# Gate and up of the second token half by seven products of quarters instead of eight

## The chip, the cores and the metric

The kernel runs on one core of one Trainium2 chip. The metric is the device time of one execution in microseconds (us). Before the change the median of three runs is 1322.51 us (1320.72 to 1323.11).

## What is computed

One encoder layer on 1024 tokens of width 1024, all in float32. The change lies in its last part, the feed-forward network (FFN) with a hidden width of 2816:

```python
x = x + jnp.concatenate([out_a, out_b], axis=-1) @ w_out[l]
h2 = rmsnorm(x, norm2_w[l])
x = x + (jax.nn.silu(h2 @ w_gate[l]) * (h2 @ w_up[l])) @ w_down[l]
```

Ahead of it stand a norm, one input projection (`w_in`), sparse attention with a top-k choice of keys, and a retention recurrence. `out_a` and `out_b` are the outputs of the last two.

## The kernel before

**Precision.** TensorE multiplies in a rounded format (`F32R`), so every operand is split in two: `hi`, the rounded copy that ScalarE (ACT) writes, and `lo`, the remainder, which VectorE (DVE) gets as source minus `hi`. A product is then three matmuls: hi times hi, hi times lo, lo times hi. Each unit of 128 rows and 128 columns of a stationary operand is loaded anew for every matmul.

**Stages.** The tokens form eight blocks of 128, in two halves of four. The stages follow one another: `in_proj(0)`, `in_proj(1)`, `out_proj(0)`, `ffn(0)`, `out_proj(1)`, `ffn(1)`. Attention, selection and retention are threads of their own that run between the matmuls of these stages; attention of the second half ends in the last group of `ffn(0)`, where `last()` waits for it and `out_prep` makes the inputs of `out_proj(1)` and loads the residual `x1` of blocks 4 to 7 (L974).

**FFN (L1013).** The split, transposed activations of a half lie in `Thi` and `Tlo` (eight slices of 128 model columns by 512 tokens). The 22 tiles of 128 hidden columns go in `groups` of 4, 4, 4, 4, 4 and 2. For a hidden tile `j`, gate and up are 2 x 8 x 3 = 48 matmuls with 512 token columns each (only tile 0 does them in two halves of 256 columns). Then the silu follows: tanh on ACT, two operations on DVE, and the split of the hidden tile, `hh` on ACT and `hl` on DVE. After a group its part of the down projection runs: per hidden tile 24 matmuls of 512 columns, and eight additions of 512 columns to `x1` for the group. In the last group each sum goes out by a DMA from ACT's queue.

**Norm (L1000).** `out_proj` (L982) goes over four chunks of `w_out`; behind the last chunk, `norm2(b)` squares and scales block `b`, and a returned function transposes it (8 matmuls against `eye`) and splits it into `Thi` and `Tlo` with eight 128-column operations on ACT and eight on DVE (`scale_in`, L328).

**Weights.** Raw weights come by SP's DMA queue into `wraw` (three buffers). `pieces` (L273) splits them in steps of 512 columns per partition into a pair `whi`, `wlo`, of which there are two (L261). `weights()` (L912) hands out the pair that is ready and starts the next chunk's filling, so the kernel works exactly one chunk ahead: a chunk can be split only when the matmuls of the chunk before last have read their pair. A gate and up chunk is one hidden tile.

**Order.** Filling a chunk is a thread (`w`) that `tick()` (L872) steps between matmuls, by a model of the engines' backlog (`charge`, L800). The framework that turns these calls into instructions then orders each engine's instructions; the rows show that this order is not that of the calls. Memory comes from pools: `per` lives through the kernel, `s12` and `s34` are the stages' own. PSUM (eight banks) has three banks `d` for products, three `t`, and two for `l` in the second stage pool.

Of the kernel before, what the change touches and what calls it, by code (L numbers as in the profile page):

```python
# [16 lines left out]
NB = 8  # L17
KT = 8
H = 8
# [99 lines left out]
class Layer:  # L119
    def __init__(self, tc, a, out, stack):  # L120
# [9 lines left out]
        self.per = pool("per", bufs=1)  # L130

# [18 lines left out]

    def st(self, shape, dt=F32, tag=None, bufs=1):
        return self.new(self.stage, shape, dt, tag, bufs)
# [4 lines left out]
    def junk(self):  # L157
        return self.sb([128, 1024], BF16, tag="junk")
# [53 lines left out]
    def constants2(self):  # L212
# [14 lines left out]
        self.bits = self.sb([128, 32], U32, tag="bits")  # L227
# [4 lines left out]
    def bias_tables(self):  # L232

        nc, a = self.nc, self.a
        far = self.sb([128, 8], tag="far")
        nc.scalar.dma_start(far, a["rel_bias"][15:16, :].to_broadcast([128, 8]))
        bias = self.sb([128, H, 256], tag="bias")
# [35 lines left out]
    def pieces(self, loads, step, n, rows):  # L273
# [7 lines left out]
        def fill():  # L281
            late = None
            for i, parts in enumerate(loads):
# [4 lines left out]
                raw = self.sb([128, 1024], tag=tag, bufs=bufs)[:, :step * n].rearrange("p (k n) -> p k n", n=n)  # L288
# [6 lines left out]
                for k0 in range(0, step, sub):  # L295
# [9 lines left out]
                    yield  # L305
            late()
# [33 lines left out]
    def x_load(self, b, queues):  # L340
        xr = self.xr[b] = [self.sb([128, 512], tag="mb_", bufs=8) for _ in range(2)]
# [61 lines left out]
    def post_idx(self, b, p):  # L403
# [6 lines left out]
        if b >= 2:  # L410
            self.iq[b] = self.sb([128, 128], tag="iq", bufs=4)
            nc.vector.tensor_copy(self.iq[b], ci[:, 128:256])
# [41 lines left out]
    def post_q(self, b, c, p):  # L454
        nc = self.nc
        if c == 0:
            self.until(lambda: b < 4 or b - 4 in self.qused, *self.threads)
            self.q[b] = self.sb([128, 512], tag="q", bufs=4)
# [116 lines left out]
    def scores(self, b):  # L575
# [4 lines left out]
        dup = self.sb([128, 512], tag="rl", bufs=2)  # L580
# [7 lines left out]
        iqT = self.sb([128, 512], F32R, tag="iqT", bufs=1)  # L588
# [6 lines left out]
        sc = self.sb([128, 1024], tag="sc", bufs=2)[:, :n]  # L595
        self.sc[b] = sc
        for c0 in range(0, n, 512):
            w = min(512, n - c0)
            for h in range(4):
                p = self.pt(w)  # L600
                nc.tensor.matmul(p, iqT[:, h * 128:h * 128 + 128], self.ikT[:, c0:c0 + w], start=True, stop=True)
                rl = self.sb([128, 512], tag="rl", bufs=2)[:, :w]
# [76 lines left out]
    def attention(self, b):  # L679
# [6 lines left out]
        qT = self.sb([128, 1024], F32R, tag="qT", bufs=1)  # L686
# [22 lines left out]
        for hp in range(H // 2):  # L709
            bias = self.bias[:, 2 * hp:2 * hp + 2, 256 - near:]  # L710
            if b >= 2:
                mb = self.sb([128, 2, 256], tag="mb")
# [27 lines left out]
            for j0 in range(0, b + 1, 2):  # L740
# [6 lines left out]
                ph = self.sb([128, 512], F32R, tag="ph", bufs=2)[:, :nj * 256]  # L747
                plo = self.sb([128, 512], F32R, tag="plo", bufs=2)[:, :nj * 256]
# [11 lines left out]
        wide = self.sb([128, 512], tag="rl", bufs=2)  # L760
# [10 lines left out]
    def heads_out(self, b, hp, pa):  # L771
# [3 lines left out]
        t = self.sb([128, 128], tag="oT")  # L775
# [120 lines left out]
    def plan(self):  # L896
# [77 lines left out]
    def out_prep(self, b):  # L974
# [3 lines left out]
        self.x1[b] = [self.mtile("ma", b), self.mtile("mb", b)]  # L978
        for s in range(2):
            nc.sync.dma_start(self.x1[b][s], self.x[b * 128:(b + 1) * 128, 512 * s:512 * s + 512])  # L980

    def out_proj(self, half):  # L982
        nc = self.nc
        bs = [4 * half + i for i in range(4)]
        late = []
        for c in range(4):
            w = self.weights()
            for b in bs:
# [5 lines left out]
                if c == 3:  # L994
                    late.append(self.norm2(b))
                    if b % 4 in (1, 2, 3):
                        late.pop(0)()
        return late

    def norm2(self, b):  # L1000
# [8 lines left out]
        for s in range(2):  # L1009
            nc.vector.tensor_scalar(xn[:, 512 * s:512 * s + 512], x1[s], rs, None, op0=OP.mult)  # L1010
        return lambda: [self.transpose_in(xn[:, 512 * g:512 * g + 512], b % 4, g, self.n2) for g in range(2)]

    def ffn(self, half, late, last):  # L1013
        nc = self.nc
        for j0, g in self.groups:
# [25 lines left out]
            for c in range(2):  # L1041
                hi, lo = self.weights()
                for t0 in (0, 2):
                    ps = [self.pd(), self.pd()]
                    for js in (range(g - 1), range(g - 1, g)):
                        for i in range(2):
                            ts = slice(128 * (t0 + i), 128 * (t0 + i) + 128)
                            for j in js:
                                nc.tensor.matmul(ps[i], hh[:, j, ts], hi[:, j, :], start=(j == 0), stop=False)
                                nc.tensor.matmul(ps[i], hh[:, j, ts], lo[:, j, :], start=False, stop=False)  # L1050
# [107 lines left out]
```

## Time and profile before

| | |
|---|---|
| median of 3 runs | 1322.51 us |
| the profiled execution | 1322.34 us, of which the span of its instructions 1320.6 us |
| TensorE matmuls (PE) | 1290.5 us busy, 98% |
| weight loads (PEld) | 1119.0 us, 85%, beside the matmuls |
| VectorE (DVE) | 889.4 us, 67% |
| ScalarE (ACT) | 723.3 us, 55% |
| GpSimd (POOL) | 57.5 us, 4% |
| granted TensorE clock | 0.998 of full speed |
| second `out_proj` | from 895.1 us, second FFN from 944.6 us to the end |

Busy times overlap. A matmul's duration holds its way through the array, so matmuls that follow one another overlap too, and the pace of a run of them (its length over its count) says what one costs. All instructions carry the line of a helper, L99, so rows are told apart by the names of their tiles.

### The profile page before, as it was taken

The page shows a single profiled execution, that of the slowest core. Times are in us where ns is not written, and L with a number is a line of the kernel's source. Part 1 is how long each engine was busy: PE and PEld are TensorE (multiplying, and loading weights), DVE is VectorE, ACT ScalarE, POOL GpSimd, SP SyncE. Part 2 cuts the span into 40 slices and gives each one's busy share as a digit, 9 for nine tenths or more (in the row PEclk, how much of TensorE's full clock was granted, in tenths as well). Part 3 has the DMA queues.
Part 4 walks back from the last instruction along what each step waited for, and adds up shares of the span by engine and source line. Part 5 has one row for each costly group of instructions (what it writes and reads, how often), then busy time and mean ns, then how long its engine had stood idle before and what let it go on. Part 6 is the DMA issues. An engine that isn't in the chain of part 4 may idle for free.

```text
span 1320.6 us, 21083 instructions
## 1 busy us (share of the span) xinstructions
PE 1290.5 (98%) x7619; PEld 1119.0 (85%) x7619; DVE 889.4 (67%) x2536; ACT 723.3 (55%) x1706; POOL 57.5 (4%) x68
## 2 busy tenths in 40 slices
PE   8799998999999999999999999999999999999998
PEld 7799898999999978888888878889988888888886
DVE  6679899789978877877887775554634343434343
ACT  7778877556685787578569734332532323232221
POOL 1401011010020000000000000000000000000000
PEclk9999999999999999999999999999999999999999
DMA  8433224221341322322322232245233333333331
GB/s 276 145 81 97 58 62 111 65 65 33 93 122 59 89 65 87 96 64 65 96 75 78 72 89 72 64 128 177 72 105 96 96 96 96 94 91 94 90 93 66
DMA packets 157785, 121.24 MB, mean 92 GB/s; under 512 B 8176, under 2 KB 137840, under 8 KB 157552
## 3 DMA queue, kind: packets, MB, share of 16 engines
q1 hardware_dynamic: 151744, 111.14, 28.8%
q10 hardware_dynamic: 5936, 8.74, 1.9%
q8 instruction: 60, 0.98, 0.3%
q14 instruction: 45, 0.37, 0.1%
HBM read 115.67 MB, written 4.19 MB: 91 GB/s over the span
## 4 chain that ended last, share of the span: by engine, by line
PE 74%; DVE 12%; ACT 8%; issue 2%; DMA 2%; POOL 2%; ACTq 0%; SPq 0%; DVEq 0%; POOLq 0%
PE d L99 64%; PE t L99 8%; ACT junk L99 3%; DVE wlo L99 2%; PE l L99 2%; DVE L L99 1%; ACT whi L99 1%; ACT Thi L99 1%; DMA bias<-in_near_dram 1%; ACT waste L99 1%; DVE zqk L99 0%; DVE plo L99 0%; DMA mb__101<-in_xt_dram 0%; DVE junk L99 0%; DVE tr L99 0%
## 5 line engine op out<-in xcount | busy, mean ns | idle before, releaser
L99 ACT ACTIVATE whi<-wraw 128x512 fp32r<-128x512 f32 (+1 forms) x388 | 220.7, 617 | 253.5 <-PE d L99 181.9
L99 PE MATMUL d<-Thi,whi 128*128 128x512 f32 (+1 forms) x736 | 284.7, 387 | 0.0
L99 PE MATMUL d<-whi,Thi 128*128 128x256 f32 (+1 forms) x960 | 281.6, 294 | 3.1 <-ACT Thi L99 1.2
L99 PE MATMUL d<-Tlo,whi 128*128 128x512 f32 (+1 forms) x736 | 283.9, 386 | 0.5 <-DVE Tlo L99 0.4
L99 PE MATMUL d<-Thi,wlo 128*128 128x512 f32 (+1 forms) x736 | 283.7, 386 | 0.0
L99 PE MATMUL d<-wlo,Thi 128*128 128x256 f32 (+1 forms) x960 | 272.3, 284 | 1.4 <-DVE wlo L99 1.3
L99 PE MATMUL d<-whi,Tlo 128*128 128x256 f32 (+1 forms) x960 | 272.1, 284 | 0.0
L99 DVE TENSOR_TENSOR wlo<-wraw,whi 128x512 fp32r<-128x512 f32 (+1 forms) x390 | 251.9, 677 | 6.5 <-ACT whi L99 5.6
L99 PEld LDWEIGHTS d<-whi,Thi 128*128 128x128 f32 x960 | 182.2, 190 | 7.8 <-ACT Thi L99 2.1
L99 PEld LDWEIGHTS d<-wlo,Thi 128*128 128x128 f32 x960 | 182.4, 190 | 3.2 <-DVE wlo L99 2.3
L99 ACT ACTIVATE junk<-sc,tc 128x384 bf16<-128x384 f32 (+5 forms) x186 | 163.6, 879 | 34.2 <-DVE tc L99 30.2
L99 PEld LDWEIGHTS d<-whi,Tlo 128*128 128x128 f32 x960 | 182.1, 190 | 0.0
L99 PEld LDWEIGHTS d<-Thi,wlo 128*128 128x128 f32 x736 | 138.2, 188 | 30.1
L99 PEld LDWEIGHTS d<-Tlo,whi 128*128 128x128 f32 x736 | 138.4, 188 | 28.6 <-DVE Tlo L99 1.1
L99 PEld LDWEIGHTS d<-Thi,whi 128*128 128x128 f32 x736 | 138.1, 188 | 28.1 <-ACT Thi L99 0.3
L99 PE MATMUL d<-whi,hh 128*128 128x512 f32 x352 | 140.1, 398 | 0.9 <-DVE mb__5825 L99 0.9
L99 PE MATMUL d<-wlo,hh 128*128 128x512 f32 x352 | 139.1, 396 | 0.0
L99 PE MATMUL d<-whi,hl 128*128 128x512 f32 x352 | 138.7, 396 | 0.0
L99 DVE TENSOR_TENSOR th<-th,d 128x512 f32<-128x512 f32 x44 | 30.2, 685 | 98.2 <-PE d L99 98.1
L99 PEld LDWEIGHTS d<-whi,hh 128*128 128x128 f32 x352 | 66.1, 188 | 16.8 <-DVE mb__5825 L99 1.4
L99 PEld LDWEIGHTS d<-whi,hl 128*128 128x128 f32 x352 | 66.1, 188 | 16.0
L99 PEld LDWEIGHTS d<-wlo,hh 128*128 128x128 f32 x352 | 66.2, 188 | 15.0
(304 smaller groups left out, 1731.7 us busy)
## 6 DMA issues: line engine op xcount, KB each, us to landing
wraw<-in_w_gate_dram SPq DMA_DIRECT2D x88, 256.0 KB, 3.1
wraw<-in_w_up_dram SPq DMA_DIRECT2D x88, 256.0 KB, 3.5
wraw<-in_w_down_dram SPq DMA_DIRECT2D x44, 512.0 KB, 3.9
wraw<-in_w_in_dram SPq DMA_DIRECT2D x24, 512.0 KB, 3.8
wraw<-in_w_in_dram SPq DMA_DIRECT2D x32, 256.0 KB, 3.4
wraw<-in_w_out_dram SPq DMA_DIRECT2D x16, 512.0 KB, 4.1
maA<-in_x_dram SPq DMA_DIRECT2D x20, 256.0 KB, 5.1
wraw<-in_w_in_dram SPq DMA_DIRECT2D x7, 292.0 KB, 3.3
```

The source lines that it names most:

```text
L99: return f(*args, **kw)
```

## The change

For the second half gate and up go by Strassen's scheme (its form with fifteen additions). For a pair of hidden tiles the weights are taken as two by two quarters (512 model columns by 128 hidden columns, gate beside up) and the activations as two by two quarters (512 model columns by 256 tokens). Seven products of sums of quarters stand in for the eight products of quarters; each has 2 x 4 x 3 = 24 matmuls with 256 token columns. The activations' sums and splits are made once, in `Phi` and `Plo` (seven each, by `turned`). The weights' sums are made per pair by `factor`, and each factor is split in one operation of 1024 columns on ACT and one on DVE; a chunk of weights is two factors. Products are partly added up in PSUM and partly by copies on ACT and additions on DVE. The raw quarters come as 512-column `quad` tiles, six buffers, by the same number of bytes as before. `hh` and `hl` now lie, twice, in the memory of `Thi` and `Tlo`. Blocks go through `out_proj` in the order 4, 6, 5, 7. `ffn(0)` stays as it was; its down projection becomes the function `down`, with the same lines.

Tiles of attention and of the earlier stages move from `per` to a pool `early`, which ends with `ffn(0)`; a new stage pool `s5` takes its memory. `x1` of blocks 4 to 7 has tiles of its own in `s5`, and its eight loads are called behind `ffn(0)` instead of within its last group. PSUM has six banks `d` and two `t` in the new stage. In the diff below, further tiles that only change `sb` into `at_` are left out.

```diff
+    def at_(self, shape, dt=F32, tag=None, bufs=1):
+        return self.new(self.early, shape, dt, tag, bufs)
...
+    def quad(self, pr, n):
+        got = self.quads.setdefault(pr, [])
+        while len(got) < n and pr < NH // 2:
+            r, c = divmod(len(got), 2)
+            q = self.st([128, 2, 4, 128], tag="quad", bufs=6)
+            for u, w in enumerate((self.w_gate, self.w_up)):
+                self.nc.sync.dma_start(q[:, u], w[512 * c:512 * c + 512, 256 * pr + 128 * r:256 * pr + 128 * r + 128]
+                                       .rearrange("(k p) n -> p k n", p=128))
+            got.append(q)
+        return got
+    def factor(self, pr, m):
+        nc = self.nc
+        q = self.quad(pr, 4)
+        if m == 0:
+            self.quad(pr + 1, 2)
+        new = lambda: self.st([128, 2, 4, 128], tag="S", bufs=2)
+        add = lambda out, a, b, op: nc.vector.tensor_tensor(out, a, b, op=op)
+        if m == 2:
+            self.s1, self.s2 = new(), new()
+            add(self.s1, q[2], q[3], OP.add)
+            add(self.s2, self.s1, q[0], OP.subtract)
+            return self.s2
+        if m == 3:
+            return self.s1
+        if m == 4:
+            s3 = new()
+            add(s3, q[0], q[2], OP.subtract)
+            return s3
+        if m == 5:
+            add(self.s2, q[1], self.s2, OP.subtract)
+            return self.s2
+        return q[{0: 0, 1: 1, 6: 3}[m]]
...
+    def chunk_parts(self, items):
+        nc = self.nc
+        hi, lo = [t[:, :1024 * len(items)].rearrange("p (i u k n) -> p i u k n", u=2, k=4, n=128) for t in self.wpair()]
+        def fill():
+            late = None
+            for i, (pr, m) in enumerate(items):
+                if late:
+                    late()
+                src = self.factor(pr, m)
+                nc.scalar.activation(hi[:, i], src, AF.Copy)
+                late = lambda i=i, src=src: nc.vector.tensor_tensor(lo[:, i], src, hi[:, i].bitcast(F32), op=OP.subtract)
+                if m in (5, 6):
+                    self.quad(pr + 1, m - 2)
+                yield
+            late()
+        return (hi, lo), fill()
...
-                for j in range(g):
-                    yield gu(j0 + j)
+                if half == 0:
+                    for j in range(g):
+                        yield gu(j0 + j)
+                else:
+                    parts = [(j0 // 2 + i, m) for i in range(g // 2) for m in range(7)]
+                    for i in range(0, len(parts), 2):
+                        yield lambda i=i, parts=parts: self.chunk_parts(parts[i:i + 2])
...
-        self.x1[b] = [self.mtile("ma", b), self.mtile("mb", b)]
+    def x1_load(self, b, tiles):
+        self.x1[b] = tiles
...
+            self.nc.sync.dma_start(self.x1[b][s], self.x[b * 128:(b + 1) * 128, 512 * s:512 * s + 512])
...
-                    late.append(self.norm2(b))
-                    if b % 4 in (1, 2, 3):
+                    late.append(norm(b))
+                    if len(late) > 1:
...
+        if b >= 4:
+            return lambda: self.turned(b, xn)
...
+    def split_part(self, m, t, src):
+        c = slice(128 * t, 128 * t + 128)
+        self.nc.scalar.activation(self.Phi[:, m, :, c], src, AF.Copy)
+        self.nc.vector.tensor_tensor(self.Plo[:, m, :, c], src, self.Phi[:, m, :, c].bitcast(F32), op=OP.subtract)
+    def turned(self, b, xn):
+        nc = self.nc
+        x = self.st([128, 8, 128], tag="cc", bufs=2)
+        for g in range(2):
+            p = self.pt()
+            for k in range(4):
+                nc.tensor.transpose(p[:, k * 128:k * 128 + 128], xn[:, 512 * g + k * 128:512 * g + k * 128 + 128], self.eye)
+            nc.vector.tensor_tensor(x[:, 4 * g:4 * g + 4, :], p.rearrange("p (k n) -> p k n", n=128),
+                                    self.n2[:, 4 * g:4 * g + 4, None].to_broadcast([128, 4, 128]), op=OP.mult)
+        if b < 6:
+            self.xa = x
+            for g in range(2):
+                self.split_part(g, b - 4, x[:, 4 * g:4 * g + 4, :])
+            return
+        (a1, a2), (b1, b2) = [(y[:, 0:4, :], y[:, 4:8, :]) for y in (self.xa, x)]
+        t1, t2, t3, t4 = [self.st([128, 4, 128], tag=n) for n in ("u2", "u3", "p5", "th")]
+        sub = lambda out, p, q: nc.vector.tensor_tensor(out, p, q, op=OP.subtract)
+        sub(t1, b1, a1)
+        sub(t2, b2, t1)
+        self.split_part(2, b - 6, t2)
+        self.split_part(3, b - 6, t1)
+        sub(t3, b2, b1)
+        self.split_part(4, b - 6, t3)
+        sub(t4, a2, t2)
+        self.split_part(5, b - 6, b2)
+        self.split_part(6, b - 6, t4)
...
+    def gate_up(self, part, late, hh, hl):
+        nc = self.nc
+        flat = lambda c: c.rearrange("p i n -> p (i n)")
+        two = lambda p: p.rearrange("p (u n) -> p u n", n=256)
+        keep = lambda name: self.st([128, 2, 256], tag=name)
+        for m in range(7):
+            hi, lo = part()
+            if m in (0, 1, 3):
+                bank = two(self.pd())
+                if m == 0:
+                    X = bank
+                if m == 3:
+                    Z = bank
+            else:
+                bank = Z if m == 5 else X
+            for u in range(2):
+                for k in range(4):
+                    first = m in (0, 1, 3) and u == 0 and k == 0
+                    for i, (w, t) in enumerate(((hi, self.Phi), (hi, self.Plo), (lo, self.Phi))):
+                        nc.tensor.matmul(bank[:, u, :], w[:, u, k, :], t[:, m, k, :], start=first and i == 0,
+                                         stop=(k == 3 and i == 2), skip_group_check=True)
+                    self.tick()
+                if m == 1 and u == 0 and late:
+                    late.pop(0)()
+            self.evacuate()
+            if m == 0:
+                p1 = keep("p1")
+                nc.scalar.activation(p1, X, AF.Copy)
+            elif m == 1:
+                c1 = self.st([128, 2, 2, 256], tag="cc", bufs=2)
+                nc.vector.tensor_tensor(c1[:, :, 0, :], bank, p1, op=OP.add)
+            elif m == 2:
+                u2 = keep("u2")
+                nc.scalar.activation(u2, X, AF.Copy)
+            elif m == 3:
+                p5 = keep("p5")
+                nc.scalar.activation(p5, Z, AF.Copy)
+            elif m == 4:
+                u3 = keep("u3")
+                nc.scalar.activation(u3, X, AF.Copy)
+                c2 = self.st([128, 2, 2, 256], tag="cc", bufs=2)
+                nc.vector.tensor_tensor(c2[:, :, 1, :], u3, p5, op=OP.add)
+            elif m == 5:
+                nc.vector.tensor_tensor(c1[:, :, 1, :], Z, u2, op=OP.add)
+                self.silu(flat(c1[:, 0]), flat(c1[:, 1]), hh[:, 0, :], hl[:, 0, :])
+            else:
+                nc.scalar.activation(c2[:, :, 0, :], X, AF.Copy)
+                self.silu(flat(c2[:, 0]), flat(c2[:, 1]), hh[:, 1, :], hl[:, 1, :])
...
+    def ffn_fast(self, late):
+        both = [self.sb([128, 4096], F32R, tag=t).rearrange("p (i j n) -> p i j n", i=2, n=512) for t in ("Thi", "Tlo")]
+        for i, (j0, g) in enumerate(self.groups):
+            hh, hl = [t[:, i % 2] for t in both]
+            ready = []
+            def part():
+                if not ready:
+                    hi, lo = self.weights()
+                    ready.extend((hi[:, i], lo[:, i]) for i in range(hi.shape[1]))
+                return ready.pop(0)
+            for pr in range(g // 2):
+                self.gate_up(part, late, hh[:, 2 * pr:2 * pr + 2, :], hl[:, 2 * pr:2 * pr + 2, :])
+            self.down(1, j0, g, hh, hl)
...
+        with sbuf("early") as self.early:
+            with sbuf("s12") as self.stage, psum("p12") as self.ps:
+                self.first_stages()
+            with sbuf("s34") as self.stage, psum("p34") as self.ps:
+                self.nd, self.nt = 3, 3
+                self.lmax = 1024
+                for b in range(4, NB):
+                    self.ma[b] = self.mtile("ma", b)
+                    self.go("att", self.attention(b))
+                late = self.out_proj(range(4), self.norm2)
+                self.ffn(0, late, lambda: (self.drain("sel", "att"), [self.out_prep(b) for b in range(4, NB)]))
+        with sbuf("s5") as self.stage, psum("p5") as self.ps:
+            self.nd, self.nt = 6, 2
+            for b in range(4, NB):
+                self.x1_load(b, [self.st([128, 512], tag="x1", bufs=8) for _ in range(2)])
+            self.Phi = self.st([128, 7, 4, 256], F32R, tag="Phi")
+            self.Plo = self.st([128, 7, 4, 256], F32R, tag="Plo")
+            late = self.out_proj((4, 6, 5, 7), self.norm2)
+            self.ffn_fast(late)
...
+        self.kkhi = self.at_([128, 1024], F32R, tag="kkhi")
+        self.kklo = self.at_([128, 1024], F32R, tag="kklo")
+        self.ikT = self.at_([128, 1024], F32R, tag="ikT")
+        self.V = self.at_([128, NB, 128], F32R, tag="V")
```

## Rows read from the trace of the kernel before

**Rows 1.** Page, part 1: busy time, share of the span, instructions.
```profile
PE 1290.5 (98%) x7619; PEld 1119.0 (85%) x7619; DVE 889.4 (67%) x2536; ACT 723.3 (55%) x1706; POOL 57.5 (4%) x68
```

**Rows 2.** Windows: length, then busy time (instructions) of each engine, granted clock, DMA.
```profile
150.00:200.00 50.00, 47.60 (x389) 45.06 (x387) 46.52 (x191) 40.99 (x122) 4.19 (x4) 1.00 0.23 67
250.00:300.00 50.00, 50.00 (x419) 48.05 (x417) 42.33 (x150) 26.45 (x81) 4.20 (x4) 1.00 0.23 64
300.00:350.00 50.00, 49.42 (x403) 47.10 (x403) 46.31 (x176) 29.64 (x84) 4.15 (x4) 1.00 0.20 54
1000.00:1100.00 100.00, 100.00 (x430) 80.47 (x429) 42.25 (x66) 25.96 (x47) 0.00 (x0) 1.00 0.33 95
```

**Rows 3.** Chain that ended last, pieces: start, us, what.
```profile
379.54 2.81 PE d L99 x24
...
617.92 28.00 PE d L99 x120
...
943.55 1.01 PE t L99 x8
944.56 5.39 PE d L99 x45
```

**Rows 4.** Groups of PE by form: busy us, mean ns of one; idle before.
```profile
L99 PE MATMUL d<-Thi,whi 128*128 128x512 f32 x672 | 266.7, 397 | 0.0
...
L99 PE MATMUL d<-whi,Thi 128*128 128x256 f32 x896 | 260.9, 291 | 0.0
```

**Rows 5.** Page, part 5: weight loads of the 256-column matmuls.
```profile
L99 PEld LDWEIGHTS d<-whi,Thi 128*128 128x128 f32 x960 | 182.2, 190 | 7.8 <-ACT Thi L99 2.1
```

**Rows 6.** Groups of DVE by form.
```profile
L99 DVE TENSOR_TENSOR wlo<-wraw,whi 128x512 fp32r<-128x512 f32 x376 | 246.0, 685 | 6.5 <-ACT whi L99 5.6
...
L99 DVE TENSOR_TENSOR bias<-bias,far 128x1024 f32<-128x1024 f32 x2 | 2.4, 1222 | 4.5 <-DMA bias<-in_near_dram 4.5
```

**Rows 7.** Groups of ACT by form.
```profile
L99 ACT ACTIVATE whi<-wraw 128x512 fp32r<-128x512 f32 x376 | 215.9, 623 | 250.9 <-PE d L99 179.6 <-issue 60.5 <-DMA out_dram<-mb__5876 4.7
```

**Rows 8.** DVE in order of time, one hidden tile of the second half.
```profile
1014.32 2.50 DVE L99 TENSOR_TENSOR wlo<-wraw,whi 128x512 fp32r<-128x512 f32 x4
...
1025.45 1.29 DVE L99 TENSOR_TENSOR wlo<-wraw,whi 128x512 fp32r<-128x512 f32 x2
1026.65 0.69 DVE L99 SCALAR_TENSOR_TENSOR hl<-th,hh 128x512 fp32r<-128x512 f32 x1
```

**Rows 9.** ACT in order of time, the same stretch.
```profile
1013.65 2.20 ACT L99 ACTIVATE whi<-wraw 128x512 fp32r<-128x512 f32 x4 [8.96 <-PE d L99]
1019.24 0.60 ACT L99 ACTIVATE th<-d 128x512 f32<-128x512 f32 x1 [3.40 <-PE d L99]
1024.61 1.15 ACT L99 ACTIVATE whi<-wraw 128x512 fp32r<-128x512 f32 x2 [4.77 <-PE d L99]
1025.67 0.61 ACT L99 ACTIVATE hh<-th 128x512 fp32r<-128x512 f32 x1
```

**Rows 10.** Waits: who for whom, us in total, times, longest.
```profile
DVE th L99 <- ACT th L99: 69.9, 31, 3.7
```

**Rows 11.** DVE in order of time, between the second out_proj and its FFN.
```profile
938.16 0.48 DVE L99 TENSOR_SCALAR wraw<-mb__10993,rs 128x512 f32<-128x512 f32 x1
938.56 2.15 DVE L99 SCALAR_TENSOR_TENSOR Tlo<-t,n,Thi 128x128 fp32r<-128x128 f32 x8
940.62 0.42 DVE L99 TENSOR_TENSOR mb__11006<-d,mb__11006 128x256 f32<-128x256 f32 x1
```

**Rows 12.** PE in order of time, the same place.
```profile
952.00 0.39 PE L99 MATMUL d<-Tlo,whi 128*128 128x256 f32 x1 [0.42 <-DVE Tlo L99]
```

**Rows 13.** SP queue in order of time, around the end of the first FFN.
```profile
880.94 1.53 SPq L99 DMA_DIRECT2D maB<-in_x_dram  x3
```

**Rows 14.** DMA issues 875 to 960 us: KB each, median us to landing.
```profile
maB<-in_x_dram SPq DMA_DIRECT2D x4, 256.0 KB, 3.8
...
out_dram<-mb__5988 ACTq DMA_DIRECT2D x1, 256.0 KB, 5.3
```

More of the change, by code (lines that the diff above doesn't have):

```diff
@@ L130, in __init__ @@
         self.per = pool("per", bufs=1)
+        self.early = None
     def new(self, pool, shape, dt, tag, bufs):
@@ L157, in junk @@
     def junk(self):
-        return self.sb([128, 1024], BF16, tag="junk")
+        return self.at_([128, 1024], BF16, tag="junk")
     def waste(self, n):
@@ L340, in x_load @@
     def x_load(self, b, queues):
-        xr = self.xr[b] = [self.sb([128, 512], tag="mb_", bufs=8) for _ in range(2)]
+        xr = self.xr[b] = [self.at_([128, 512], tag="mb_", bufs=8) for _ in range(2)]
         for s in range(2):
@@ L977, in out_prep, with out_proj @@
         self.transpose_in(self.mb[b], b % 4, 1)
-        self.x1[b] = [self.mtile("ma", b), self.mtile("mb", b)]
+    def x1_load(self, b, tiles):
+        self.x1[b] = tiles
         for s in range(2):
-            nc.sync.dma_start(self.x1[b][s], self.x[b * 128:(b + 1) * 128, 512 * s:512 * s + 512])
-    def out_proj(self, half):
+            self.nc.sync.dma_start(self.x1[b][s], self.x[b * 128:(b + 1) * 128, 512 * s:512 * s + 512])
+    def out_proj(self, bs, norm):
         nc = self.nc
-        bs = [4 * half + i for i in range(4)]
         late = []
@@ L1040, in ffn @@
                 last()
[L1041 to L1050, printed above, removed]
-                                nc.tensor.matmul(ps[i], hl[:, j, ts], hi[:, j, :], start=False, stop=(j == g - 1))
-                                self.tick()
-                    self.evacuate()
-                    for i in range(2):
-                        b = 4 * half + t0 + i
-                        xs = self.x1[b][c]
-                        nc.vector.tensor_tensor(xs, ps[i], xs, op=OP.add)
-                        if j0 == self.groups[-1][0]:
-                            nc.scalar.dma_start(self.out[0, b * 128:(b + 1) * 128, 512 * c:512 * c + 512], xs)
@@ new lines, in ffn, with down @@
+            self.down(half, j0, g, hh, hl)
+    def down(self, half, j0, g, hh, hl):
+        nc = self.nc
+        for c in range(2):
+            hi, lo = self.weights()
+            for t0 in (0, 2):
+                ps = [self.pd(), self.pd()]
+                for js in (range(g - 1), range(g - 1, g)):
+                    for i in range(2):
+                        ts = slice(128 * (t0 + i), 128 * (t0 + i) + 128)
+                        for j in js:
+                            nc.tensor.matmul(ps[i], hh[:, j, ts], hi[:, j, :], start=(j == 0), stop=False)
+                            nc.tensor.matmul(ps[i], hh[:, j, ts], lo[:, j, :], start=False, stop=False)
+                            nc.tensor.matmul(ps[i], hl[:, j, ts], hi[:, j, :], start=False, stop=(j == g - 1))
+                            self.tick()
+                self.evacuate()
+                for i in range(2):
+                    b = 4 * half + t0 + i
+                    xs = self.x1[b][c]
+                    nc.vector.tensor_tensor(xs, ps[i], xs, op=OP.add)
+                    if j0 == self.groups[-1][0]:
+                        nc.scalar.dma_start(self.out[0, b * 128:(b + 1) * 128, 512 * c:512 * c + 512], xs)
@@ L1111, in body @@
-        with self.tc.tile_pool(name="s34", bufs=1, reuse_waits="tile") as self.stage, \
-                self.tc.tile_pool(name="p34", bufs=1, space=PSUM, reuse_waits="tile") as self.ps:
-            self.nd, self.nt = 3, 3
-            self.lmax = 1024
-            for b in range(4, NB):
-                self.ma[b] = self.mtile("ma", b)
-                self.go("att", self.attention(b))
-            late = self.out_proj(0)
-            self.ffn(0, late, lambda: (self.drain("sel", "att"), [self.out_prep(b) for b in range(4, NB)]))
-            late = self.out_proj(1)
-            self.ffn(1, late, lambda: None)
+        from contextlib import ExitStack
```

97 lines of the change are left out of this document (53 added, 44 removed).

## The prediction

> **What bounds the kernel now.** I read the page's busy table first [rows 1]: the reader is to see PE at 98% and the next engine, DVE, at 67%. A busy share can hide waits, so I read the windows next [rows 2]. From 1000 to 1100 us, inside the second FFN, PE is busy for the whole stretch at full granted clock, with DVE at 42% and ACT at 26%. Third, the chain of waits [rows 3]: it runs through PE alone there, so a matmul's price is its pace. 120 matmuls of 512 columns take 28.00 us, 233.3 ns each; 24 of 256 columns take 2.81 us, 117.1 ns each, half. The groups by form [rows 4] give means of 397 and 291 ns, far over these paces, because neighbours overlap; no sum is made from them. The second FFN begins at 944.56 us [rows 3] and its 22 x (48 + 24) matmuls of 512 columns need 1584 x 0.2333 = 369.5 us, so it would end at 1314.1 without any wait; the span is over at 1320.6, with the last additions and stores behind the last matmul. Hence this stage is TensorE's, and removing matmuls there is worth their pace as long as DVE and ACT keep up. That is the whole question.
>
> **What is removed.** A pair of hidden tiles has 96 matmuls of 512 columns now, 96 x 0.2333 = 22.40 us. It gets 7 x 24 = 168 of 256 columns, 168 x 0.1171 = 19.67 us. The difference, 2.73 us, times 11 pairs is **-30.0 us**. The pace of a 256-column matmul in this pattern (a new stationary operand for each) is that of `out_proj`, whose matmuls load one each as well.
>
> The row of the loads [rows 5] has 190 ns for a load, more than the 117 ns from one matmul to the next, so loads overlap and did not set the pace there. The Trainium skill speaks against the exchange: "TensorE: Matmul & The Clock Gate", section "Back-to-back issue gap", puts a sustained stream of loads and matmuls at about 81 ns for 128 columns and 131 ns for 512, by which halving the columns saves far less than half. A straight line between these, an estimate from that page, gives 98 ns for 256 columns, so 16.4 us for the new pair against 12.6 for the old, and about 42 us lost instead of 30 gained. This trace disagrees with it, at 233.3 against 117.1 ns.
>
> **What DVE gets.** A split of 512 columns takes 685 ns, an operation of 1024 takes 1222 ns [rows 6]. In a row, four take 2.50 us [rows 8], so each but the first costs (2.50 - 0.69) / 3 = 0.605 us; the 1024-column one, 0.537 us longer, 1.14. A pair now costs DVE 8 splits and 6 silu operations, 14 x 0.605 = 8.5 us. It will cost 7 splits and 4 weight sums of 1024 columns, 11 x 1.14 = 12.6, and 3 sums and 6 silu operations of 512, 9 x 0.605 = 5.4: 18.0 us, against PE's 19.67. That is 92% in this stage. On ACT a split of 512 columns takes 623 ns [rows 7] and one more in a row (2.20 - 0.62) / 3 = 0.53 us [rows 9]; seven splits of 1024, at twice this, and nine operations of 512 are 12.2 us of 19.67, so ACT isn't the bound. During down (22.4 us per group of four) DVE has about 16 x 0.605 = 9.7 us of work, but its spare time helps little, because the split runs one chunk ahead at most.
>
> What DVE at 92% makes PE lose, no row of this stage shows. The nearest rows are earlier stretches with DVE at 93, 85 and 93% [rows 2]: PE loses 2.40, 0.00 and 0.58 us of 50, a mean of 2.0%. On 11 x 19.67 = 216.4 us that is **+4.3 us**; bounds 0 and 4.8%, 10.4 us.
>
> It matters here in what order DVE takes its work, since a silu has two places where it waits for ACT. The code calls `hh` and `hl` directly behind the product, before the next chunk's splits are even begun; yet ACT runs two `whi` of that chunk ahead of `hh` [rows 9], and DVE puts two `wlo` before `hl` [rows 8]. So the finished order fills such gaps with ready work, which is why I take the mean and not more.
>
> **The start of the stage.** Today a block's transposed tile costs DVE 2.15 us [rows 11]. `turned` makes that 4 x 0.605 = 2.4 us for blocks 4 and 5, and 11 x 0.605 = 6.7 for 6 and 7 (two scalings, four sums, five splits). Now what must be done before the seventh product of the first pair: the third projected block (5) 2.4, blocks 6 and 7 13.4, the last two blocks' additions and scalings about 2 x 1.5 (0.42 and two of 0.48, less overlap, and the small ones) [rows 11], nine weight operations for products 3 to 7 10.3, two sums 1.2: 30.3 us. It starts when block 6, second in line, is transposed. The trace has the second block's eight operations at 938.56, which is about that time; the end is then 968.9 at the earliest. Without waits the seventh product would start at 944.6 (the first matmul of the FFN), plus 1.0 for the last transposes [rows 3], plus 6 x 2.81: 962.5. So PE waits 6.4 us. Two weight sums (2.3 us) need only loaded quarters and can go earlier: 4.1. Today's wait at this place is one of 0.42 us that the row shows [rows 12] and about as much before it, so 3.3 to 5.6 us are added. I take **+5 us**, near the upper end, since block 6's sums are called ahead of block 5's splits, for which product 1 waits; bounds 3 and 8.5 (all of them ahead of it).
>
> **The end of a group.** `hh` of the last tile now comes after the sum, the tanh and the silu: 3 x 0.69 on DVE, 0.60 and 0.62 on ACT [rows 6, 7, 9], 3.3 us behind its product. In groups of four, down has three earlier tiles, 18 matmuls and 4.2 us, to hide it: nothing. In the last group there is one earlier tile, whose own chain ends 3.3 - 2.81 = 0.5 us after the last product, and six matmuls of 1.4 us. **+1.5 us**, bounds 0 and 3.
>
> **The rest.** The loads keep their bytes and their size. `x1` moves behind the first FFN in the code; its loads are issued at 880.9 us today [rows 13], about 17 us before the first addition needs them. Their new memory is the first 16 KB of the new pool, which the first tiles of `early` held (keys and values, four of 4 KB, dead when attention ends); I take 0, cover being that wait-free memory and six PSUM banks, 6 x 2.81 = 16.9 us of products. The first half keeps its instructions: 0.
>
> **Sum.** -30.0 + 4.3 + 5 + 1.5 = -19.2, from the profiled execution's 1322.34 us (span 1320.6 and 1.7 around it; the runs' median is 1322.51): about **1303 us**. By the bounds: -30 + 0 + 3 + 0 = -27, 1295; -30 + 10.4 + 8.5 + 3 = -8, 1314.
>
> **Rivals.** *The order on DVE goes wrong (slower).* If the silu stands in DVE's queue as the code calls it, DVE stops for tanh and for `hh`, 0.60 + 0.62 and some 0.1 of signalling, and up to a 1024-column split (1.06) before each of the two on ACT: 1.3 to 3.4 us per silu. Two per pair make DVE's 18.0 into 20.6 to 24.8, 0.9 to 5.1 over PE's 19.67, middle 3.0. With start and end that is -30 + 33 + 6.5 = +9.5: 1332 us. It is slower from (30 - 6.5) / 11 = 2.1 us per pair on. For it: DVE does stand still for the tanh, 69.9 us in all [rows 10], though with nothing else to do; against it, the order seen above. The skill's page named above says, under "Architectural detail", that the queues of both engines are strictly first in, first out, which is what this rival needs; the rows don't contradict it.
>
> *The seam between two pairs.* In the chunk that holds product 7 of one pair and product 1 of the next, DVE has two silus and their sum (7 x 0.605 = 4.2) and the next chunk's two sums and splits (4.6): 8.8 us against 5.62, 3.2 too much if nothing is brought forward. Five groups have one such seam: 16 us in place of the 4.3: 1315. With every bound of start and end it is 1320.
>
> *`x1` comes late.* If its tiles lie where a stored result still waits, it is loaded after the last store: the last product's end near 895, an addition and issue of about 2, 5.3 and 3.8 [rows 14] make 906; the first addition would wait some 8 us, of which the banks hide nearly all, but splits queued behind it could cost 3: 1306.
>
> *The pace does not halve* beside so busy a DVE. If a load's 190 ns [rows 5] set it, a pair would take 31.9 us, 9.5 more than now, and the kernel about 1427. It is slower from 22.40 / 168 = 133 ns on.
>
> **Chances.** Forecast 0.58; `x1` late 0.05; seam 0.17 (0.12 faster, 0.04 the same, 0.01 slower); order 0.17 (0.02 the same, 0.15 slower); pace 0.03. Within 0.2% (2.6 us) is what a measurement of this kernel can't tell from no change. Faster 0.75, same 0.06, slower 0.19. The likeliest case's own range is 1295 to 1314; to leave out no more than 2 in 10, the range goes up through the seam and the mild end of the order: 1295 to 1326.
>
> **What would show it.** Gate and up of the second half have 22 x 48 + 48 (tile 0 in halves) = 1104 matmuls and get 1848, so PE has 7619 + 744 = 8363 in all. Right: the chain stays on PE in the second FFN; 256-column matmuls there at 117 ns; PE idle of about 1% to 3% in gate and up, put down to `wlo`; a gap of 4 to 8 us behind the second `out_proj`, put down to `Plo` or `Phi`; DVE near 90% between downs, about 1000 us in all. Wrong: PE waits for `wlo` of over 2 us in each pair while DVE idles on `th` or `hl` (order), a wait once per group (seam), DVE or PE idle on a load of `x1` near 900, or a 256-column pace over 120 ns. A first half that ends later than 895 us would be a cause that I haven't named.

## The result and the profile after

The changed kernel takes 1301.03 us (median of four runs, 1298.79 to 1301.61) against 1322.61 (1320.72 to 1323.11) for the kernel before: a ratio of 0.9836, 95% interval 0.9819 to 0.9853. The profiled execution took 1298.79 us, its span 1297.0.

The busy table, to be set against [rows 1]: TensorE has the 8363 matmuls that were forecast, DVE rose by 115 us.

```profile
PE 1258.3 (97%) x8363; PEld 1131.0 (87%) x8363; DVE 1004.1 (77%) x2600; ACT 782.2 (60%) x1732; POOL 58.2 (4%) x68
```

The first half kept its time: the second `out_proj` starts at 895.2 us, as before. From its first matmul to the kernel's last, the starts of the matmul records lie 420.96 us apart before and 397.69 after. I split this by the times from one start to the next: those over 0.345 us are gaps (a matmul of 512 columns takes 0.233), the others count for the matmul that they follow.

| us | before | after |
|---|---|---|
| gate and up without gaps | 246.9 | 211.5 |
| every gap of TensorE in this stretch | 2.0 | 14.2 |
| the rest (projection, transposes, down) | 172.1 | 172.1 |

So 35.4 us went and 12.2 came back. The windows (columns as in [rows 2]) show where they are not: inside the stage TensorE is busy throughout, although DVE went from 42% to 73%, and to 85% in the last stretch.

```profile
945.00:950.00 5.00, 0.00 (x0) 0.00 (x0) 5.00 (x10) 3.02 (x7) 0.00 (x0) 0.69 0.35 105
950.00:955.00 5.00, 4.54 (x25) 4.29 (x26) 4.52 (x8) 0.95 (x2) 1.00 (x1) 0.63 0.00 0
951.30:953.70 2.40, 2.40 (x12) 2.40 (x12) 2.12 (x4) 0.00 (x0) 0.25 (x1) 0.50 0.00 0
...
1050.00:1100.00 50.00, 50.00 (x340) 45.30 (x340) 36.72 (x45) 21.90 (x32) 0.00 (x0) 1.00 0.32 95
...
1200.00:1250.00 50.00, 50.00 (x388) 47.40 (x387) 42.60 (x51) 26.38 (x38) 0.00 (x0) 1.00 0.32 95
```

The gaps sit at the start. TensorE in order of time; the bracket is the idle time before and what ended it (the last row is the end of the last group):

```profile
943.69 1.07 PE L99 MATMUL t<-eye,wraw 128*128 128x128 f32 x8 [0.65 <-DVE wraw L99]
950.47 1.12 PE L99 MATMUL d<-Phi,whi 128*128 128x256 f32 x2 [5.71 <-ACT Phi L99]
951.38 0.41 PE L99 MATMUL d<-Plo,whi 128*128 128x256 f32 x1
951.59 0.41 PE L99 MATMUL d<-Phi,wlo 128*128 128x256 f32 x1
...
953.83 0.28 PE L99 MATMUL d<-Plo,whi 128*128 128x256 f32 x1
953.95 0.29 PE L99 MATMUL d<-Phi,wlo 128*128 128x256 f32 x1
...
956.35 1.04 PE L99 MATMUL t<-eye,wraw 128*128 128x128 f32 x8
...
960.99 0.91 PE L99 MATMUL d<-Phi,whi 128*128 128x256 f32 x2 [2.23 <-ACT Phi L99]
...
1281.82 0.50 PE L99 MATMUL d<-whi,Thi 128*128 128x512 f32 x1 [1.25 <-ACT Thi L99]
```

The first product waits 5.71 us, the third 2.23. Between them the matmuls begin 0.21 us apart, then 0.12: in the first two windows the granted clock averages 0.69 and 0.63, as it passes from the 2.4 GHz level to that of 1.2 GHz and back, and from 951.3 to 953.7 us it is 0.50. TensorE had stood idle since the transposes of 943.69. Eleven intervals of 0.213 us (from 951.38 to 953.72) instead of 0.117 cost 1.1 us more.

The bracket names ACT, which was waiting itself. The chain of waits tells for what:

```profile
943.05 0.88 DVE wraw L99 x2
943.94 0.60 DVE u L99
944.54 0.60 DVE Plo L99
945.14 0.60 DVE p L99
945.74 0.60 DVE th L99
946.34 2.41 DVE Plo L99 x4
948.75 0.34 DVE x L99
949.09 1.19 DVE cc L99 x2
...
955.34 2.27 DVE S L99 x2
957.61 1.21 DVE cc L99 x2
...
958.84 0.63 ACT Phi L99
959.47 0.95 ACT whi L99
960.41 1.05 ACT Phi L99 x2
...
961.51 149.28 PE d L99 x1102
```

From 943 to 950 us it is DVE alone: block 6's sums (`u`, `p`, `th`) and splits (`Plo`) run ahead of the scaling (`cc`, 949.09) of block 5's transposed tile, on which the first product waits. The transposes of that block had been through since 944.8 (943.69 and 1.07 in the rows above). From 961.51 on, 1102 matmuls in a row with no wait between them.

The loads of `x1` did come late. On SP's queue they stood behind loads of `w_out` that waited for a `wraw` buffer, and DVE's first additions waited 4.97 + 2.28 + 0.58 = 7.8 us for them:

```profile
873.01 25.38 SPq L99 DMA_DIRECT2D wraw<-in_w_out_dram  x5
898.48 5.81 SPq L99 DMA_DIRECT2D x<-in_x_dram  x8
```

TensorE shows no wait there.

### The profile page after: what moved, and what is told of

Its sections match the earlier page's. It is cut to its first block, busy times and chain, and to the rows that moved or that the text cites. A ratio compares the mean times of both kernels' runs of the same rounds, so it can differ in the third digit from the quotient of the medians.

```text
span 1297.0 us, 22620 instructions
## 1 busy us (share of the span) xinstructions
PE 1258.3 (97%) x8363; PEld 1131.0 (87%) x8363; DVE 1004.1 (77%) x2600; ACT 782.2 (60%) x1732; POOL 58.2 (4%) x68
## 4 chain that ended last, share of the span: by engine, by line
PE 70%; DVE 14%; ACT 10%; issue 3%; POOL 2%; DMA 1%; SPq 0%; ACTq 0%; POOLq 0%; DVEq 0%
PE d L99 60%; PE t L99 8%; ACT junk L99 4%; DVE wlo L99 2%; PE l L99 2%; DVE L L99 2%; ACT whi L99 2%; ACT Thi L99 1%; DMA bias<-in_near_dram 1%; DVE tr L99 0%; DVE cc L99 0%; DVE junk L99 0%; DVE maA L99 0%; DVE zqk L99 0%; POOL rc L99 0%
## 5 line engine op out<-in xcount | busy, mean ns | idle before, releaser
L99 PE MATMUL d<-whi,Thi 128*128 128x256 f32 (+2 forms) x1136 | 352.6, 311 | 5.5 <-ACT Thi L99 3.6
L99 PE MATMUL d<-wlo,Thi 128*128 128x256 f32 (+2 forms) x1136 | 342.7, 302 | 1.5 <-DVE wlo L99 1.4
L99 PE MATMUL d<-whi,Tlo 128*128 128x256 f32 (+2 forms) x1136 | 342.5, 302 | 0.0
L99 PE MATMUL d<-Phi,whi 128*128 128x256 f32 x616 | 171.7, 279 | 8.1 <-ACT Phi L99 7.9
L99 PE MATMUL d<-Plo,whi 128*128 128x256 f32 x616 | 171.0, 278 | 0.0
L99 PE MATMUL d<-Phi,wlo 128*128 128x256 f32 x616 | 170.8, 277 | 0.0
L99 PE MATMUL d<-Thi,whi 128*128 128x512 f32 (+1 forms) x368 | 143.3, 390 | 0.0
L99 PE MATMUL d<-Tlo,whi 128*128 128x512 f32 (+1 forms) x368 | 141.9, 386 | 0.1
L99 PE MATMUL d<-Thi,wlo 128*128 128x512 f32 (+1 forms) x368 | 141.8, 385 | 0.0
L99 PEld LDWEIGHTS d<-Phi,whi 128*128 128x128 f32 x616 | 116.4, 189 | 9.2 <-ACT Phi L99 9.0
```

Source lines behind the costliest of these rows:

```text
L99: return f(*args, **kw)
```

## The experiments

Each edit is made to the changed kernel. "Over the changed kernel" compares with its 1301.03 us; the ratio is that to the kernel before in the same runs. The changed kernel itself was not run again beside the experiments, and the kernel before took 1320.88 to 1321.36 us there against 1322.61 beside the changed kernel. Set against the changed kernel's 0.9836, the ratios therefore put every edit some 1 to 2 us slower than the medians do.

| run | us | ratio, 95% interval |
|---|---|---|
| e1 eighth product | 1329.82 | 1.0066, 1.0046 to 1.0087 |
| e2 four useless sums | 1317.54 | 0.9977, 0.9962 to 0.9992 |
| e3 eight useless sums | 1322.30 | 1.0006, 0.9995 to 1.0016 |
| e7 pools only | 1321.35 | 0.9999, 0.9990 to 1.0009 |
| e4 order 4, 5, 6, 7 | 1301.68 | 0.9854, 0.9839 to 0.9868 |
| e5 scaling on ACT | 1300.76 | 0.9845, 0.9830 to 0.9860 |
| e8 both | 1299.79 | 0.9837, 0.9821 to 0.9853 |
| e6 factors shifted | 1300.28 | 0.9842, 0.9822 to 0.9862 |
| e9 five splits less | 1296.60 | 0.9816, 0.9801 to 0.9830 |
| e10 lo twice | 1307.76 | 0.9897, 0.9881 to 0.9914 |
| e11 sums on GpSimd | 1304.34 | 0.9876, 0.9861 to 0.9891 |
| e12 order, GpSimd | 1303.51 | 0.9867, 0.9852 to 0.9882 |

**Is it the matmuls? e1** computes product 4 a second time into a spare bank, which makes eight products again.

```diff
+            if m == 3:
+                spare = two(self.pd())
...
+                            nc.tensor.matmul(spare[:, u, :], w[:, u, k, :], t[:, m, k, :], ...)
```

> The changed kernel plus 24 matmuls of 256 columns per pair (product 4 of 7 once more, into a PSUM bank that nobody reads; the result stays the same). Theory: TensorE bounds gate and up, so an eighth product costs its pace, 11 x 24 x 0.114 to 0.117 = 30.1 to 30.9 us, 1331 to 1332 us. Rival: DVE sets the pace of gate and up; then the extra matmuls fill PE's gaps, and the cost is under 15 us.

It cost 28.8 us over the changed kernel for 264 matmuls, 0.109 each; by the ratios 30.4 us, 0.115 each, which is the theory's price. The rival's 15 us is far off. The product that is saved is thus more than the whole gain: with all of the scheme's additions and eight products the kernel is slower than before.

**Is it the pools? e7** keeps the old gate and up in both halves, and moves the pools, the banks and the loads of `x1` only. Further lines that drop `turned`, `Phi` and `Plo` are left out here.

```diff
-                if half == 0:
+                if True:
...
-            late = self.out_proj((4, 6, 5, 7), self.norm2)
-            self.ffn_fast(late)
+            late = self.out_proj(range(4, NB), self.norm2)
+            self.ffn(1, late, lambda: None)
```

> The new pools, the new place of the x1 loads and the six PSUM banks alone: the second half's gate and up go by the old eight products, with 512 columns. Theory: the pools move no time, 1320 to 1325 us, ratio 0.998 to 1.002. Rival one: the banks or the free hh buffers bring part of the gain, under 1318 us. Rival two: the late x1 loads (DVE waits 7.8 us for them) cost what the products give back, over 1326 us.

No difference that can be measured. In this kernel the loads of `x1` are free, late or not.

**How near is DVE to being the bound? e2 and e3** add sums of 512 columns that nobody reads to each pair, four at two products, or eight at four.

```diff
+        if m in (1, 4):
+            for u in range(2):
+                add(self.waste(512).rearrange("p (k n) -> p k n", n=128), q[0][:, u], q[1][:, u], OP.add)
```

> The changed kernel plus four useless DVE additions of 512 columns per pair (2.4 us), whose results nobody reads. DVE's sum per pair goes from 18.0 to 20.4 us, over PE's 168 x 0.114 = 19.2. Theory: DVE's 92% is hidden up to PE's time, so only the excess shows, 1.2 us x 11 = 13 us at most, 1304 to 1314 us. Rival: waits between DVE and ACT have used up DVE's spare time, so all 2.4 x 11 = 27 us show, 1328 us.

> The changed kernel plus eight useless DVE additions of 512 columns per pair (4.8 us): 22.8 us of DVE against 19.2 of PE. Theory: the excess shows, 3.6 x 11 = 40 us, less what the first chunk of a group gains during down: 1330 to 1341 us. Rival (spare time already used up): 4.8 x 11 = 53 us, 1354 us. If DVE has far more room than I counted: under 1315 us.

They cost 16.5 and 21.3 us. The first four lie between their theory (at most 1314 us) and their rival (1328); with eight the time is under the theory's range and over 1315, so none of the three forecasts of e3 came. TensorE's waits in e2 from 965 us on (total, times, longest) are behind ACT's copies, not behind `wlo`. The last row is a wait of DVE itself:

```profile
PE d L99 <- ACT Thi L99: 5.6, 6, 1.2
PE d L99 <- ACT p L99: 5.5, 5, 1.4
...
DVE waste L99 <- DMA quad<-in_w_gate_dram: 5.7, 4, 1.5
```

The useless sums read raw quarters, and DVE stands in front of them for the loads. With its other waits for quarters that makes 15.8 us from 965 us on, against 10.0 in the changed kernel and 3.6 in e10. So part of e2's cost can be a wait for loads; how much was not measured. Work without a reader is a poor gauge, as it can bring in waits of its own and the finished order may put it anywhere. **e10** therefore repeats work with a deadline, the low part of two factors of a pair:

```diff
-                late = lambda i=i, src=src: nc.vector.tensor_tensor(lo[:, i], ...)
+                late = lambda i=i, m=m, src=src: [nc.vector.tensor_tensor(lo[:, i], ...)
+                                                  for _ in range(2 if m in (1, 4) else 1)]
```

> The low parts of two of the seven factors of a pair (products 2 and 5) are computed twice into the same place, 2 x 1.14 = 2.3 us more of DVE work per pair that the next product must wait for, 20.3 us against TensorE's 19.2 at the pace of the changed kernel. Theory: what counts is DVE's total against TensorE's in gate and up, so 1.1 us x 11 = 12 us at most, less what down's spare time gives back: 1304 to 1313. Rival: the useless additions cost 16.5 us because of the place at which they stood in DVE's queue; then work that stands directly in front of a product costs as much or more, up to 22 x 1.14 = 25 us: 1317 to 1326.

It cost 6.7 us (8.1 by the ratios), of 22 x 1.14 = 25 us of work: inside the theory's range, and under the rival's. Now TensorE does wait for `wlo`, 0.8 us at most:

```profile
PE d L99 <- DVE wlo L99: 3.5, 5, 0.8
```

So the changed kernel, at 18.0 of 19.2 us per pair by the count, stands below the point at which DVE's total counts, and in e10, whose work the products need, the total set the cost and not the place in front of a product. In its profiled execution some 2.4 us of the cost are no wait but a slower pace, 0.1154 us per matmul instead of 0.1141, for which see the last heading.

**What sets the start? e4** takes the blocks in the order 4, 5, 6, 7 (block 5 ahead of block 6's sums); **e5** gives the scaling of the transposed tiles to ACT; **e8** does both. Further lines of e4 and e8, which keep blocks 4 and 5 in two of the `quad` buffers, are left out.

```diff
-            late = self.out_proj((4, 6, 5, 7), self.norm2)
+            late = self.out_proj((4, 5, 6, 7), self.norm2)
```

```diff
-            nc.vector.tensor_tensor(x[:, 4 * g:4 * g + 4, :], p.rearrange("p (k n) -> p k n", n=128), ...)
+            for k in range(4):
+                nc.scalar.activation(x[:, 4 * g + k, :], p[:, k * 128:k * 128 + 128], AF.Identity, ...)
```

> The changed kernel with blocks in the order 4, 5, 6, 7 through the second out_proj, so that the plain splits of blocks 4 and 5, which products 1 and 2 need, come ahead of the sums of 6 and 7 (the transposed blocks 4 and 5 lie in two quad buffers, so the second pair's first quarters are loaded later). Theory: PE's first wait of 5.7 us is block 5's split standing behind block 6's eleven operations on DVE; it goes to 1 or 2 us, the matmuls at half clock behind it (about 1.4 us) go too, and the wait at product 3 grows from 2.2 to 4 or 5: 1295 to 1298 us. Rival: DVE's total of work before the seventh product sets the loss, whatever the order: 1300 to 1302 us.

> The changed kernel with the norm's weights multiplied in by ACT (eight operations of 128 columns per block) instead of DVE (two of 512). DVE has 4.8 us less to do there, ACT 8.8 more. Theory: DVE's sum is what PE waits for at the start, so the waits of 5.7 and 2.2 us shrink by 3 to 4.8 in all: 1296 to 1298 us. Rival: the splits into Phi, also on ACT, now stand behind the scalings, and nothing is won: 1300 to 1304 us.

> Both edits, order 4, 5, 6, 7 and scaling on ACT. Theory: the gains add in part, PE's waits at the start from about 11 us in all to 3 to 6: 1293 to 1297 us. Rival: one of them had taken all there was, so no better than the better of the two.

None can be told from the changed kernel, as the rival of each had it. In e4 the wait moved: block 5 is in time, and now the products behind wait for block 6 and the weights, 8.1 us in these rows against 5.71 + 2.23 = 7.9:

```profile
956.65 0.58 PE L99 MATMUL d<-Phi,whi 128*128 128x256 f32 x1 [4.21 <-ACT Phi L99]
957.80 0.58 PE L99 MATMUL d<-Plo,whi 128*128 128x256 f32 x1 [0.56 <-DVE Plo L99]
959.00 0.58 PE L99 MATMUL d<-Plo,whi 128*128 128x256 f32 x1 [0.40 <-DVE Plo L99]
962.54 0.58 PE L99 MATMUL d<-Phi,wlo 128*128 128x256 f32 x1 [2.96 <-DVE wlo L99]
```

In e5 the first wait stayed, at 5.96 us: ACT ran block 6's copies and then block 5's eight scalings (946.83 to 949.88) ahead of the copies that the first product needs.

**e9** takes work away instead: the low parts of the activations' factors 3 to 7 are not computed.

```diff
-        self.nc.vector.tensor_tensor(self.Plo[:, m, :, c], src, ...)
+        if m < 2:
+            self.nc.vector.tensor_tensor(self.Plo[:, m, :, c], src, ...)
```

> The five splits of activation sums that DVE makes for blocks 6 and 7 at the start (the low parts of products 3 to 7) are left out; constants written during the second projection stand in their place, so the low terms of these products are not computed. Theory: DVE's work in front of block 5, and then its total, sets the two waits at the start. Block 6 has then six operations there instead of eleven: 5 x 0.605 = 3.0 us off the first wait of 5.7, and the second (2.2) goes: about 1294 to 1297. Rival: the chain of block 5 itself (projection, addition, norm, transposes, ACT's rounded copies) sets the first wait; then the time stays at 1299 to 1301.

The first wait fell by 2.9 us to 2.84, about what five splits of 0.605 make: what stood in front of block 5's scaling is shown. The whole fell by 4.4 us by the medians, by 2.6 by the ratios, whose intervals overlap, and the stretch from `out_proj` to the last matmul by 1.6 only; so the wait is shown, the gain in time less surely. A second wait of 1.66 us stays, and DVE itself is idle for 1.39 us before it. Its chain:

```profile
948.82 6.20 PE d L99 x34
955.01 0.45 PE t L99 x4
...
955.49 1.30 DVE cc L99 x2
...
956.81 0.63 ACT Phi L99
957.44 0.95 ACT whi L99
958.39 0.53 ACT Phi L99
...
958.96 11.15 PE d L99 x94
```

This is a second limit, which the prediction did not have. The transposes of block 7 are called in the middle of product 2, and 3.9 us lie between them and product 3, while half a product (12 matmuls) covers 1.4. The 34 matmuls ahead took 6.20 us, where 34 x 0.1171 = 4.0 would do. Nineteen of their intervals are 0.213 us at a granted clock of 0.50, eight more than in the changed kernel, which took back 0.8 us of the gain. An earlier call of these transposes was not tried.

**e11 and e12** give the four sums to GpSimd, in the changed kernel's order and in that of e4.

```diff
-        sub = lambda out, p, q: nc.vector.tensor_tensor(out, p, q, op=OP.subtract)
+        sub = lambda out, p, q: nc.gpsimd.tensor_tensor(out, p, q, op=OP.subtract)
```

> The four sums of activations of blocks 6 and 7 go to GpSimd instead of DVE. Theory (DVE's work in front of block 5 sets the first wait): 4 x 0.605 = 2.4 us less there, the first wait falls from 5.7 to 3.3 us, the second goes: 1296 to 1299. Rival: a sum on GpSimd takes longer than on DVE and stands in the chain from block 6's sums to its rounded copies and splits, so that the splits come no earlier: 1300 to 1305.

> Blocks in the order 4, 5, 6, 7 and the four sums on GpSimd. With the order alone the first wait went and one of about as much came at product 3, for DVE's work as a whole. Theory: 2 x 2.4 us of that work are now elsewhere, so that wait shrinks by 3 to 5 us: 1296 to 1299. Rival: the chain through the sums is as long on GpSimd, product 3 waits as before: 1301 to 1304.

Both are slower, e11 by 3.3 us and e12 by 2.5 (5.3 and 4.1 by the ratios), as the rival had it. Two things are behind it. One is at the first product, and the rival did not name it. GpSimd in e11, in order of time:

```profile
940.92 1.30 POOL L99 TENSOR_TENSOR u<-cc 128x512 f32<-128x512 f32 x1 [3.20 <-DVE cc L99]
942.30 1.27 POOL L99 TENSOR_TENSOR u<-cc,u 128x512 f32<-128x512 f32 x1
943.52 0.56 POOL L99 TENSOR_TENSOR rs<-rq,half 128x1 f32<-128x1 f32 x1
944.03 1.27 POOL L99 TENSOR_TENSOR p<-cc 128x512 f32<-128x512 f32 x1
945.25 1.46 POOL L99 TENSOR_TENSOR th<-cc,u 128x512 f32<-128x512 f32 x1
...
960.70 2.12 POOL L99 TENSOR_TENSOR u<-cc,u 128x512 f32<-128x512 f32 x1
```

And DVE:

```profile
941.29 0.20 DVE L99 TENSOR_SCALAR rq<-ss 128x1 f32<-128x1 f32 x1
944.11 2.89 DVE L99 TENSOR_SCALAR wraw<-x,rs 128x512 f32<-128x512 f32 x2 [2.62 <-POOL rs L99]
```

The power of block 5's norm (`rs`) queues behind two sums, so DVE waits 2.62 us in front of that norm's scalings instead of 0.45. These then take 2.89 us instead of 0.88, beside the next sums (944.03 and 945.25). The Trainium skill ("SBUF — State Buffer", section "SBUF: two separate sides") says that GpSimd and some forms of DVE operations lock a pair of ports against each other for a whole instruction; these rows agree with it.

The other is the rival's own chain, at product 3. Block 7's second sum ends at 962.82 (the last row of GpSimd), and TensorE waits for ACT's copy of it:

```profile
963.54 0.38 PE L99 MATMUL d<-Phi,whi 128*128 128x256 f32 x1 [1.82 <-ACT Phi L99]
```

**Why are the matmuls faster? e6** shifts both parts of the factors by 32 columns in `whi` and `wlo` (the reason is under the last heading).

```diff
-        hi, lo = [t[:, :1024 * len(items)]...
+        hi, lo = [t[:, 32:32 + 1024 * len(items)]...
```

> The changed kernel with the seven factors' splits 128 bytes further on in the same buffers. It asks why the 256-column matmuls of gate and up run at two paces, 113.3 and about 117.7 ns, with a switch at waits. Theory one: the pace hangs on the addresses of the stationary operand; then nearly all go to one pace, 1299 or 1308 us. Theory two: it is a phase that a wait leaves behind; then the mix stays, a mean of 114 to 116 ns, and the time is 1300 to 1303 us.

Time and pace stayed (0.1139 us per matmul against 0.1141): a shift of 128 bytes does not change the mixture. Other places were not tried.

## Why the prediction was right

Forecast were 1303 us and a gain of 19.2; measured are 1301.03 and 21.6 by the medians (23.6 between the profiled executions). The mechanism held. Of its terms the steady state came out 3.9 us under the forecast, the start 5.6 over it and outside its bounds, and a faster pace of 5.5 us was missing. These three partly cancel, so that the total came as close as it did is in part luck. The right column adds up to -23.6 us, against 23.3 by which the stretch of TensorE shrank. The start is the added gaps less those of the steady state and the end and less the matmuls' own time in them, 9.5 us, and 1.1 us by the lower clock. Taken from start to start, the idle 1.25 us at the end is 1.4.

| term, us | forecast | measured |
|---|---|---|
| columns removed, at 0.1171 per matmul | -30.0 | -30.5 |
| a faster pace, 1848 x (0.1171 - 0.1141) | none | -5.5 |
| DVE in the steady state | +4.3 (0 to 10.4) | about +0.4 |
| start of the stage | +5 (3 to 8.5) | about +10.6 |
| end of the last group | +1.5 (0 to 3) | +1.4 |
| `x1` late, first half | 0 | 0 |

**The removal** is confirmed by e1: 28.8 to 30.4 us for the eighth product. The pace halves with the columns, 0.2333 us for 512 and 0.114 for 256. The estimate by a straight line between two figures of the Trainium skill ("TensorE: Matmul & The Clock Gate", section "Back-to-back issue gap") would have made the kernel slower; these runs disagree with it for this pattern.

**The steady state** was oversized. The waits for `wlo` that were to show in it, 1% to 3% of gate and up, do not occur: from 965 us on TensorE waits twice, both times for `hh`, 1.5 us in all, 1.25 of it at the end of the last group. The loss of 2.0% came from stretches of attention. Why it does not carry over was not tested; a likely reason is that DVE's work there sits in chains with TensorE and ACT, while here DVE works one chunk ahead for a reader that comes at a fixed pace. e10, with DVE about 6% over TensorE's time per pair (20.3 against 19.2 us), costs 6.7 us. The order rival is refuted too: DVE's waits for tanh, 69.9 us in [rows 10], fell to 13.2, and from 944 us on from 57.5 to 0.8. So is the seam: no wait once per group.

**The start** failed as a step. The prediction added up DVE's work up to product 7 and took the end of that sum as the only deadline. By it product 7 would start at 968.9; it started at 972.9. Its own remark, that block 6's sums are called ahead of block 5's splits, was the decisive matter: block 5 was added, normed and transposed by 944.8, but the sums and splits pushed back the scaling of its transposed tile to 949.09 and with it ACT's copies, so TensorE stood from the first product on. Three things then came on top: the chain from block 7's transposes to product 3 (e9), the clock at its lower level after the idle time (1.1 us), and DVE's two weight sums, behind which block 7's scalings began some 0.7 us after the first four transposes (956.35, 0.45 us for four as in e9; 957.52). e4 and e8 show that another order only moves the wait.

**The end** has the forecast size, but at another place. The wait of 1.25 us is in front of the earlier tile's `hh`, for which the prediction had 0.5 us (with the last tile's 1.4 its own rows make 1.9 us, not 1.5): on ACT a piece of weights (`whi`, 1280.54) was copied ahead of it. The last tile's chain, which was to cost the rest, shows no wait.

**`x1`** came late by the rival's mechanism, in part: the queue that held it was that of `w_out`'s loads, not a stored result. Its 7.8 us on DVE were hidden as reckoned for the main case, by banks and spare time on DVE.

## What to carry to other kernels

In a stage that TensorE bounds, trading matmul columns for additions paid here with the other engine's total at 18.0 of TensorE's 19.2 us per pair, and less so at 20.3 (e10). Its work had a reader one step later; whether the same holds for chains that go back and forth was not tested. The cost of this exchange sat at its ends. So list for the first units which operations stand in front of the first deadline, not only which are due by the last, and count each serial chain from a late transpose to its product. An experiment that loads an engine must give the extra work a deadline, and be searched for waits that this work brings in, or it measures the order of the instructions.

## What was not expected of the hardware

The matmuls of 256 columns in the new gate and up run at two paces at a granted clock of 1.00, and change between them without a wait. In the changed kernel's timeline, 24 matmuls lie between the first two rows (0.118 us each), 27 between the second and the third (0.113):

```profile
1020.02 0.28 PE L99 MATMUL d<-Phi,whi 128*128 128x256 f32 x1
...
1022.85 0.28 PE L99 MATMUL d<-Phi,whi 128*128 128x256 f32 x1
...
1025.91 0.28 PE L99 MATMUL d<-Phi,whi 128*128 128x256 f32 x1
```

The matmuls of 256 columns in the second `out_proj` stay at 0.118 in both kernels. e6 leaves the mixture as it is, and the mean goes from 0.1139 (e6) to 0.1157 (e2) between the runs; what chooses the pace stays open. On this kernel it is worth the 5.5 us of the table.

GpSimd's sums and DVE's operations took longer beside each other: in e11 a 512-column scaling on DVE 1.45 us (half of 2.89) instead of 0.44, and one of GpSimd's sums 2.12 us (960.70) instead of 1.27.
